# Down projection of a gated MLP: another order of the seven fast-multiplication products, sums left in PSUM, and every engine's order written by hand

## The chip, the core and the metric

The kernel runs on one core of a Trainium2 chip. The metric is the time of one execution on the device in microseconds (us), the median of the runs. The core has a matrix engine (PE, with weight loads shown apart as PEld), a vector engine (DVE), a scalar engine (ACT), a GpSimd engine (POOL) and a queue that starts transfers (SP). Each engine works through its own list of instructions in order. Results of PE go to PSUM, of which the kernel uses eight banks of 128 partitions by 512 float32; all other tiles lie in SBUF.

## The reference

One layer of a hybrid encoder on 1024 tokens of width 1024: a norm, a pooling and attention mixer with an output projection, a second norm, and a gated MLP with a causal convolution of width 3. The change touches only its last product and what follows:

```python
h = rmsnorm(x, norm_ffn_g)                       # x: 1024 x 1024, after the mixer
u = causal_dwconv(h @ w_up, conv_w, conv_b)      # w_up: 1024 x 5632
gate, val = jnp.split(u, 2, axis=-1)             # each 1024 x 2816
x = x + (jax.nn.silu(gate) * val) @ w_down       # w_down: 2816 x 1024
return rmsnorm(x, norm_final_g)
```

Everything is float32. A float32 product is done on PE as three fast passes: each operand is split into a high and a low part, and high*high, high*low and low*high are added in PSUM.

## The kernel before

The last 240 us are of interest. The activations `silu(gate) * val` come out of the up projection in 22 steps (`up`, lines 808 to 898), one for each 128 of the 2816 columns. A step holds seven products of 12 matmuls, for the up projection is done by Winograd's form of Strassen's scheme: seven block products in place of eight. The tail of a step (the taps of the convolution, the silu and the multiply, `after0` to `after4`, `store_a`, `store_b`) is done within the next step, and that of the last one behind it. `store_a` and `store_b` write the activations and three sums of them (S1 to S4) to DRAM.

The down projection uses the same scheme. The activations are cut into blocks A11, A12 (token rows 0 to 511), A21, A22 (rows 512 to 1023), the weight `w_down` into B11, B12, B21, B22, each 1408 by 512. Seven products P1 to P7 are computed, in the order P1, P2, P3, P7, P5, P6, P4 (line 975). Each has 11 units (one for 128 of the 1408 inner columns), and a unit is 4 row blocks of 128 tokens (j = 0 to 3) times the three passes of `mm3` (lines 78 to 81): 12 matmuls of 128 x 512, so that there are 7 x 11 x 12 = 924. For each unit `load` (line 979) fetches the left operand from DRAM into a `raw` tile and splits it and the right operand. A split (lines 83 to 91) is a copy on ACT for the high part (line 86) and a subtraction on DVE for the low part (line 87). Every split of the down projection is recorded at these two lines, the left ones under tile names such as aP59l, the right ones as `wP` or `lw`.

The right operands of P7, P5, P6 and P4 are sums of weight blocks. Each costs one POOL instruction per unit (`pool2`, line 956; P7 into a tile named T, the others in place in `B12`), 44 in all. Each product has four PSUM banks of its own, in turn from two pools (`banks`), begins them afresh, and when it is done, `evac` (line 1082) adds its four results into the tiles X of the residual, P5 and P7 into two places each. P1 is also copied into `sp`, P6 is added to it, and `sp` goes into three quarters of X later:

```python
elif p == "P5":
    into(x12(j), y)
    into(x22(j), y)
elif p == "P6":
    into(sp[j], y)
```

The final norm is woven into P4: for the upper 512 rows (`upper`, 4 steps each), for the lower ones partly (`lower`), and the rest in `last` (line 1070) after each of the last four groups of 9 matmuls: a square with its row sum on ACT, a multiply by the gain on DVE, two small POOL instructions for the scale of a row, the scaling of one half on DVE and the other on ACT, and two transfers out.

Order: during the up steps all engines follow an order written by hand (line 921). From line 928 on only SP does, and from line 1137 on PE; the other engines' instructions of the down projection are ordered by a planner, which may place them among those of the last up steps. Tiles come from rings of named tags (`BUFS`, line 62): `raw` has 4, `hi` and `lo` 5 each, `T` 5, `E` 6, `M` 8. A tile waits for the last reader of the tile that held its place before.

Of the kernel before, what the change touches and what calls it, by code (L numbers as in the profile page):

```python
# [50 lines left out]
def block_kernel(ctx, tc, x, xT, pos, wv, wqk, wp, wo, wup, wdn, cols, invf, rcnt, gffn, gfin,  # L51
# [723 lines left out]

    def store_b(u):
# [5 lines left out]
        tens(out=s34[:, H:T], in0=a[:, 0:H], in1=s12[:, H:T], op=sub)  # L782
        t = dram(f"S12{i}", s12)
# [24 lines left out]
    def up(p, u, g, h):  # L808
# [7 lines left out]
        product(x6, u.S2w, "T2", u.ahead)  # L816
        up_split(u, "S3", nc.gpsimd)
# [63 lines left out]
        if g:  # L881
            up_split(g, "S2")
        u.o1 = conv(u, 1, u.uv)
# [12 lines left out]
        tens(out=u.ug[:, H:T], in0=z, in1=u2, op=add)  # L896
        if p:
# [57 lines left out]
    def pool2(dst, a, b, op=sub):  # L955
        nc.gpsimd.tensor_tensor(out=dst, in0=a, in1=b, op=op)  # L956
        return dst

    t3 = {}

    def wside(p, i):
        if p in ("P1", "P2", "P3"):
            return wdown({"P1": "B11", "P2": "B21", "P3": "B22"}[p], i)
        if p == "P7":
            if i % 2 == 0:
                t3[0] = st("E", f"T3{i}")
            return pool2(t3[0][:, (i % 2) * H:(i % 2 + 1) * H], wdown("B22", i), wdown("B12", i))
        w = wdown("B12", i)
        if p == "P5":
            return pool2(w, w, wdown("B11", i))  # L970
        if p == "P6":
            return pool2(w, wdown("B22", i), w)
        return pool2(w, w, wdown("B21", i))

    left = {"P1": "A11", "P2": "A12", "P3": "S4", "P7": "S3", "P5": "S1", "P6": "S2", "P4": "A22"}
    lw = {}
    P1E = 6

    def load(p, i):
        late = p == "P4" and i >= NG - LAST  # L980
        r = st("raw", f"ar{p}{i}")
        nc.sync.dma_start(out=r, in_=opd[left[p], i])
        a = wsplit(r, f"a{p}{i}")
        if late:
            if 0 not in lw:
                lw[0] = [st("M", f"lw{k}", [P, 4, H], F32R) for k in range(2)]
            wh, wl = [t[:, i - NG + LAST, :] for t in lw[0]]
        elif p == "P4":
            if i % 2 == 0:
                lw["h"] = st("M", f"w{p}{i}", [P, 4, H], F32R)  # L990
            wh, wl = [lw["h"][:, i % 2 * 2 + k, :] for k in range(2)]
        elif i % 2 and (p != "P1" or i > P1E):
# [7 lines left out]
    def banks(p, k):  # L1000
        if k % 2 == 0:
            return [psB(f"d{p}{j}") for j in range(4)]
        t = [psS(f"d{p}{j}") for j in range(2)]
        return [t[j // 2][:, (j % 2) * H:(j % 2 + 1) * H] for j in range(4)]

    def unit(acc, j, i, w):
        c = slice(j * P, (j + 1) * P)
        mm3(acc[j], w[0][0][:, c], w[0][1][:, c], w[1][0], w[1][1], i == 0, i == NG - 1)

    def xb(j, n):  # L1010

        return lambda t: X[j * 4 + t][:, n * H:(n + 1) * H]

    x11, x12, x21, x22 = xb(0, 0), xb(0, 1), xb(1, 0), xb(1, 1)

    def into(x, y, op=add, eng=None):
        (eng or nc.vector).tensor_tensor(out=x, in0=x, in1=y, op=op)

    s3 = [sm.tile([P, 4], F32, name=f"s3{tt}", tag=f"s3{tt}", bufs=1) for tt in range(NT)]
    fin, gfb = {}, {}  # L1020

    def square(tt, n):
        if tt not in fin:
            fin[tt] = st("E", f"of{tt}")
        nc.scalar.activation(fin[tt][:, n * H:(n + 1) * H], X[tt][:, n * H:(n + 1) * H], AF.Square, accum_out=s3[tt][:, n:n + 1])

    def half_mean(tt, n):
        nc.gpsimd.tensor_scalar(out=s3[tt][:, 2:3], in0=s3[tt][:, n:n + 1], scalar1=1.0 / D, scalar2=EPS,
                                op0=ALU.mult, op1=ALU.add)

    def row_scale(tt, n):
        s = s3[tt]
        nc.gpsimd.tensor_scalar(out=s[:, 3:4], in0=s[:, n:n + 1], scalar1=1.0 / D, scalar2=s[:, 2:3],
                                op0=ALU.mult, op1=ALU.add)
# [164 lines left out]
```

## Time and profile before

| | us |
|---|---|
| median of 3 runs | 1057.57 |
| lowest, highest run | 1054.36, 1454.11 |
| the profiled execution | 1052.37 |
| its span, first to last instruction | 1050.6 |

The profiled execution is one run of its own. Its time is the span and 1.77 us outside it. The rows below are from its trace. Times are us from the start of the span. A duration ends when the result is written; the next instruction of the same engine can start earlier than that. "wP<-B12w,wP" reads: tile wP is written from B12w and wP. What stands behind "<-" in brackets is what ended an engine's idle time. PE's clock was granted in full (1.00) in every stretch of 30 us from 820 to 1030.

### The profile page before, as it was taken

How to read it: one execution, taken by the hardware profiler on the slowest of the kernel's cores; microseconds unless marked ns; L12 is line 12 of the kernel's file. 1: busy time of each engine (PE TensorE's matmuls, PEld its weight loads, DVE VectorE, ACT ScalarE, POOL GpSimd, SP SyncE). 2: the span in 40 equal slices, each digit the busy share in tenths (PEclk: the TensorE clock that was granted, in tenths of full speed). 3: DMA queues.
4: the chain of work that ended last, by engine and by line, in shares of the span. 5: the costliest groups of instructions: out<-in, count | busy, mean ns of one | idle time of the engine just before them, and what ended most of it. 6: DMA issues, size and time to landing. Idle time of an engine off the chain costs nothing.

```text
span 1050.6 us, 13509 instructions
## 1 busy us (share of the span) xinstructions
PE 1012.6 (96%) x4612; PEld 836.3 (80%) x4612; DVE 782.6 (74%) x1141; ACT 510.1 (49%) x896; POOL 324.9 (31%) x284
## 2 busy tenths in 40 slices
PE   8999999999998998999999999999999999999995
PEld 6888888887887876778888888888888788877884
DVE  6465887989775678587776777677676865799894
ACT  6722554447555355244445445454453654344533
POOL 0000121322121156443433333334332000775462
PEclk9999999999999999999999999999999999999998
DMA  9627543324325223232422322233233885533214
GB/s 313 234 90 279 182 141 120 102 71 141 117 95 180 80 85 113 73 136 78 139 100 81 121 101 100 101 118 113 72 131 130 299 313 207 163 120 112 91 65 176
DMA packets 67974, 143.89 MB, mean 137 GB/s; under 512 B 8513, under 2 KB 9665, under 8 KB 67905
## 3 DMA queue, kind: packets, MB, share of 16 engines
q1 hardware_dynamic: 67904, 143.03, 39.6%
q8 instruction: 36, 0.59, 0.2%
q14 instruction: 34, 0.27, 0.1%
HBM read 105.78 MB, written 37.22 MB: 136 GB/s over the span
## 4 chain that ended last, share of the span: by engine, by line
PE 70%; DVE 7%; POOL 3%; issue 3%; ACT 2%; DMA 1%; SPq 0%; POOLq 0%; DVEq 0%; ACTq 0%
PE P L81 9%; PE P L79 9%; PE P L80 9%; PE dP L80 4%; PE dP L81 4%; PE dP L79 4%; PE Z L79 4%; PE Z L80 4%; PE Z L81 4%; PE po L81 3%; PE po L79 3%; PE sc L386 2%; PE po L80 2%; PE O L433 2%; PE pp L79 1%
## 5 line engine op out<-in xcount | busy, mean ns | idle before, releaser
L403 POOL TENSOR_SCALAR e<-e,sm 128x128 f32<-128x128 f32 (+7 forms) x32 | 29.7, 932 | 174.9 <-DMA k<-tsk 68.9
L735 POOL TENSOR_TENSOR S<-wa,wa 128x512 f32<-128x512 f32 x44 | 64.7, 1490 | 0.9 <-DMA wa<-in_wup 0.9
L399 ACT ACTIVATE e<-sc,mx 128x128 f32<-128x128 f32 (+7 forms) x64 | 47.1, 741 | 32.5 <-DVE mx L389 16.7
L753 DVE SCALAR_TENSOR_TENSOR o<-ug,col,o 128x1023 f32<-128x1023 f32 (+1 forms) x44 | 56.3, 1281 | 0.0
L753 DVE SCALAR_TENSOR_TENSOR o<-uv,col,o 128x1023 f32<-128x1023 f32 (+1 forms) x44 | 56.3, 1279 | 0.0
L735 POOL TENSOR_TENSOR S<-S,wa 128x512 f32<-128x512 f32 x22 | 28.3, 1287 | 73.8 <-DVE a224l L87 4.8
L956 POOL TENSOR_TENSOR T<-B22w,B12w 128x512 f32<-128x512 f32 x11 | 19.0, 1728 | 93.3 <-DVE wP L87 93.3
L735 POOL TENSOR_TENSOR S<-wa,S 128x512 f32<-128x512 f32 x22 | 28.5, 1294 | 51.0 <-issue 50.9
L848 ACT COPY u<-P 128x512 f32<-128x512 f32 x18 | 10.6, 587 | 69.2 <-PE P L81 69.2
L386 PE MATMUL sc<-K,Q 128*128 128x512 f32 (+3 forms) x192 | 42.8, 352 | 0.3 <-ACT e L399 0.3
L386 PEld LDWEIGHTS sc<-K,Q 128*128 128x128 f32 x192 | 32.7, 190 | 5.7 <-ACT e L399 0.9
L748 ACT ACTIVATE o<-ug,col 128x1024 f32<-128x1024 f32 x22 | 26.6, 1210 | 20.1 <-DVE ug L896 20.1
L421 ACT COPY at<-tp 128x512 f32<-128x512 f32 (+3 forms) x48 | 21.6, 483 | 28.5 <-PE tp L417 28.5
L828 ACT COPY u<-P 128x512 f32<-128x512 f32 x18 | 10.6, 587 | 50.0 <-PE P L81 50.0
L433 PE MATMUL O<-at,V 128*128 128x256 f32 (+1 forms) x160 | 34.0, 358 | 0.0
L433 PEld LDWEIGHTS O<-at,V 128*128 128x128 f32 x160 | 29.8, 190 | 4.0
L564 DVE TENSOR_TENSOR X<-X,po 128x512 f32<-128x512 f32 x32 | 21.7, 682 | 14.7 <-PE po L81 14.6
L389 DVE TENSOR_REDUCE mx<-sc 128x1 f32<-128x640 f32 (+3 forms) x32 | 32.2, 1014 | 0.4
L806 DVE TENSOR_TENSOR ac<-o,g 128x1024 f32<-128x1024 f32 x22 | 26.9, 1224 | 7.1 <-ACT g L804 6.9
L748 ACT ACTIVATE o<-uv,col 128x1024 f32<-128x1024 f32 x22 | 26.7, 1214 | 9.6 <-DVE uv L878 9.6
L87 DVE TENSOR_TENSOR wP<-B12w,wP 128x512 fp32r<-128x512 f32 x30 | 26.4, 904 | 3.2 <-ACT wP L86 1.8
L867 ACT COPY s<-P 128x512 f32<-128x512 f32 x18 | 10.6, 587 | 33.1 <-PE P L81 33.1
(2479 smaller groups left out, 3561.2 us busy)
## 6 DMA issues: line engine op xcount, KB each, us to landing
wa<-in_wup SPq DMA_DIRECT2D x88, 256.0 KB, 3.3
S<-s SPq DMA_DIRECT2D x22, 512.0 KB, 3.0
arP<-S SPq DMA_DIRECT2D x44, 256.0 KB, 2.6
arP<-A SPq DMA_DIRECT2D x33, 256.0 KB, 5.0
Q<-q SPq DMA_DIRECT2D x64, 128.0 KB, 2.9
A<-ac SPq DMA_DIRECT2D x11, 512.0 KB, 2.9
xs<-in_x SPq DMA_DIRECT2D x8, 512.0 KB, 7.9
K<-k SPq DMA_DIRECT2D x8, 512.0 KB, 5.1
```

The lines of the kernel that those rows point to most:

```text
L79: mm(dst, lhi, rhi, start=first, stop=False, skip_group_check=more)
L80: mm(dst, lhi, rlo, start=False, stop=False, skip_group_check=more)
L81: mm(dst, llo, rhi, start=False, stop=last, skip_group_check=more)
L386: mm(sc[:, k0:k1], qst[h, grp][n * 2 + hl][:, qc], kst[h][n][:, k0:k1], start=hl == 0, stop=hl == 1)
L389: nc.vector.tensor_reduce(out=nmx[:, n:n + 1], in_=sc[:, 0:L], axis=AX.X, op=ALU.max, negate=True)
L399: nc.scalar.activation(ee[n], scs[n][:, 0:L], AF.Exp, bias=nmx[:, n:n + 1], accum_out=sums[:, n:n + 1])
L403: nc.gpsimd.tensor_scalar(out=e1, in0=e1, scalar1=sums[:, 3:4], scalar2=1.0, op0=ALU.mult, op1=ALU.mult)
L433: mm(O[:, c0:256], V[j][:, h * P:(h + 1) * P], at[:, j, c0:256], start=j == 0, stop=j == nj - 1)
L735: pool(out=t, in0=getattr(u, x), in1=getattr(u, y), op=op)
L748: nc.scalar.activation(o, src, AF.Identity, bias=col[:, cc + 3:cc + 4], scale=col[:, cc + 2:cc + 3])
L753: nc.vector.scalar_tensor_tensor(out=o[:, d:T], in0=src[:, 0:T - d], scalar=col[:, cc + 2 - d:cc + 3 - d], in1=o[:, d:T], op0=ALU.mult, op ...
L806: tens(out=p.act, in0=p.o1, in1=g, op=ALU.mult)
```

## The change

The seven products are done in the order P1, P2, P6, P5, P3, P7, P4. P1, P6, P7 and P4 use the same four banks (`xb`): P6, P7 and P4 don't begin them afresh, but go on adding, so that the banks hold P1, then P1+P6, then P1+P6+P7, then all four. P2 and P5 begin the other four banks (`zb`), and P3 adds on P5. After each product the present content of its banks is added into one place of X, 28 additions in all; `sp` and its copies are gone. P4's right operand has the opposite sign, so it is added.

The weight sums are differences now, made on DVE. During P2, B11 becomes B12-B11 (the right operand of P5). In P6, t = B22-B11, with that new B11, is the right operand, and B21 becomes B21-t (that of P4). During P3, B12 becomes B22-B12 (that of P7). That is 44 DVE instructions of 128 x 512 in SBUF: two for each unit of P6, one for each of P2 and of P3.

Every engine follows the program's order, from the first up step to the end. `prepare(k)` issues ahead: weights 5 units ahead, left operands (`fetch`) one unit before their splits (`load`), splits two units before PE needs them. The first left operands and weights are asked for inside the last up step (`first_weights(0)`), and the splits of units 0 to 4 are placed within it and between the last taps. The last activations' sums and their stores are made after units 3 and 6. X is loaded in P1 (rows 0 to 511) and in P6. The norm of the upper rows is done during P7, a first part of the lower ones during P4, and the rest after each group of 9 matmuls in two pieces: `last1` of one block comes before `last2` of the block ahead of it.

The diff, without the bodies that it moves unchanged and with its long removed stretches cut:

```diff
-        t = dram(f"A2{i}", a)
-        opd["A12", i], opd["A22", i] = t[:, 0:H], t[:, H:T]
+        if u is not us[-1]:
+            store_out1(u)
         acts["s12"] = st("E", f"s12{i}")
         tens(out=acts["s12"][:, 0:H], in0=acts[i][:, H:T], in1=a[:, H:T], op=add)
...
         s12, s34 = acts["s12"], acts["s34"]
         tens(out=s12[:, H:T], in0=s12[:, 0:H], in1=acts[i][:, 0:H], op=sub)
         tens(out=s34[:, H:T], in0=a[:, 0:H], in1=s12[:, H:T], op=sub)
+        if u is not us[-1]:
+            store_out2(u)
+    def store_out1(u):
+        i = u.f % NG
+        t = dram(f"A2{i}", u.act)
+        opd["A12", i], opd["A22", i] = t[:, 0:H], t[:, H:T]
+    def store_out2(u):
+        i, s12, s34 = u.f % NG, acts["s12"], acts["s34"]
...
-    def up(p, u, g, h):
+    def up(p, u, g, h, also=None):
...
+        if also:
+            also(0)
...
+        if also:
+            also(3)
...
+        if also:
+            also(1)
         u.o1 = conv(u, 1, u.uv)
         if p:
...
+        if also:
+            also(2)
...
-    with tc.manual_schedule(engines={E.PE, E.Activation, E.DVE, E.Pool, E.SP}):
...
+    t2 = {}
     def wside(p, i):
-        if p in ("P1", "P2", "P3"):
-            return wdown({"P1": "B11", "P2": "B21", "P3": "B22"}[p], i)
-        if p == "P7":
+        if p == "P6":
             if i % 2 == 0:
-                t3[0] = st("E", f"T3{i}")
...
+                t2[0] = st("E", f"T2{i}")
+            t = t2[0][:, (i % 2) * H:(i % 2 + 1) * H]
+            tens(out=t, in0=wdown("B22", i), in1=wdown("B11", i), op=sub)
+            tens(out=wdown("B21", i), in0=wdown("B21", i), in1=t, op=sub)
+            return t
+        return wdown({"P1": "B11", "P2": "B21", "P5": "B11", "P3": "B22", "P7": "B12", "P4": "B21"}[p], i)
+    def sums(p, i):
+        if p == "P2":
+            tens(out=wdown("B11", i), in0=wdown("B12", i), in1=wdown("B11", i), op=sub)
+        if p == "P3":
+            tens(out=wdown("B12", i), in0=wdown("B22", i), in1=wdown("B12", i), op=sub)
...
+    left = {"P1": "A11", "P2": "A12", "P6": "S2", "P5": "S1", "P3": "S4", "P7": "S3", "P4": "A22"}
+    raws, early, lw = {}, [], {}
+    def fetch(p, i):
+        r = raws[p, i] = st("raw", f"ar{p}{i}")
+        nc.sync.dma_start(out=r, in_=opd[left[p], i])
...
+    def into(j, n, y):
+        x = X[j][:, n * H:(n + 1) * H]
+        tens(out=x, in0=x, in1=y, op=add)
+    def evac(p, j, y):
+        if p in ("P1", "P2"):
+            into(j, 0, y)
+        elif p in ("P6", "P3"):
+            into(j, 1, y)
+        elif p in ("P5", "P7"):
+            into(4 + j, 1, y)
+        else:
+            into(4 + j, 0, y)
...
+    def last1(tt):
+        s = s3[tt]
         square(tt, 0)
         gain(tt, 0)
-        row_scale(tt, 0)
+        mean(s[:, 3:4], s[:, 0:1], s[:, 2:3])
+        power(s[:, 3:4])
+    def last2(tt):
...
+            emit(tt, halves[n])
...
+    todo = {}
     for j in range(4):
         for step in range(4):
-            todo[j + step].append((upper, j, step))
...
+            todo.setdefault(("P7", 1 + 2 * j + step), []).append((upper, j, step))
+        for step in range(2):
+            todo.setdefault(("P4", 1 + j + step), []).append((lower, 4 + j, step))
+    DEEP, WAHEAD = 3, 5
+    units = [(p, i) for p in left for i in range(NG)]
+    wneed = {"P1": ("B11",), "P2": ("B21", "B12"), "P6": ("B22",)}
+    xload = {("P1", 5 + k): k for k in range(4)}
+    xload.update({("P6", 4 + k): 4 + k for k in range(4)})
+    ready, ahead = {}, [0, 0, 0]
+    def prepare(k):
+        while ahead[2] < min(k + WAHEAD, len(units)):
+            p, i = units[ahead[2]]
+            for nm in wneed.get(p, ()):
+                wdown(nm, i)
+            ahead[2] += 1
+        while ahead[0] < min(k + 2, len(units)):
+            n = units[ahead[0]]
+            fetch(*n)
+            if n in xload:
+                load_x(xload[n])
+            ahead[0] += 1
+        while ahead[1] < min(k + 1, len(units)):
+            n = units[ahead[1]]
+            ready[n] = load(*n)
+            sums(*n)
+            ahead[1] += 1
+    def first_weights(step):
+        if step:
+            prepare((0, 1, 2, 0)[step])
+            return
+        early.extend(st("M", f"we{k}", [P, 4, H], F32R) for k in range(2))
+        for n in range(4):
+            fetch(*units[n])
+            wdown("B11", n)
+        ahead[0] = 4
+        for i in range(4, 8):
+            wdown("B11", i)
+    E = mybir.EngineType
+    ctx.enter_context(tc.manual_schedule(engines={E.PE, E.Activation, E.DVE, E.Pool, E.SP}))
+    for n in range(NF):
+        up(us[n - 1] if n else None, us[n], us[n + 1] if n + 1 < NF else None, us[n + 2] if n + 2 < NF else None,
+           first_weights if n == NF - 1 else None)
+    after0(us[-1])
+    prepare(3)
+    after1(us[-1])
+    after2(us[-1])
+    prepare(4)
+    after3(us[-1])
+    after4(us[-1])
...
+    xb = [psB(f"x{j}") for j in range(4)]
+    k = 0
+    for p in left:
+        if p in ("P2", "P5"):
+            t = [psS(f"d{p}{j}") for j in range(2)]
+            zb = [t[j // 2][:, (j % 2) * H:(j % 2 + 1) * H] for j in range(4)]
+        acc = zb if p in ("P2", "P5", "P3") else xb
+        more = p in ("P6", "P7", "P4", "P3")
         for i in range(NG - LAST if p == "P4" else NG):
-            while queue and len(ready) < DEEP:
...
+            prepare(k + DEEP - 1)
             w = ready.pop((p, i))
             for j in range(4):
-                unit(acc, j, i, w)
...
+                unit(acc, j, w, i == 0 and not more, i == NG - 1, more)
+                if i == NG - 1:
+                    if acc is xb:
+                        evac(p, j, acc[j])
+                    elif j % 2:
+                        evac(p, j - 1, acc[j - 1])
+                        evac(p, j, acc[j])
+            for fn, j, step in todo.get((p, i), ()):
+                fn(j, step)
+            k += 1
+            if k == 4:
+                store_a(us[-1])
+                store_b(us[-1])
+            if k == 7:
+                store_out1(us[-1])
+                store_out2(us[-1])
+        if p == "P6":
+            for n, nm in enumerate(("B21", "B12")):
+                gfb.append(wblk[nm][:, 3, :])
+                nc.sync.dma_start(out=gfb[n], in_=gfin[halves[n]].partition_broadcast(P))
+    prepare(len(units))
+    ws = [ready[("P4", i)] for i in range(NG - LAST, NG)]
+    for j in range(5):
+        if j < 4:
+            for n in range(LAST):
+                unit(xb, j, ws[n], False, n == LAST - 1, True)
+            evac("P4", j, xb[j])
+            last1(4 + j)
+        if j:
+            last2(3 + j)
```

## Rows read from the trace of the kernel before

**Rows 1.** The page: span, and busy time of each engine with its share.
```profile
span 1050.6 us, 13509 instructions
PE 1012.6 (96%) x4612; PEld 836.3 (80%) x4612; DVE 782.6 (74%) x1141; ACT 510.1 (49%) x896; POOL 324.9 (31%) x284
```
**Rows 2.** Busy times by stretch: PE, PEld, DVE, ACT, POOL, then clock, DMA.
```profile
850.00:880.00 30.00, 30.00 (x134) 24.86 (x133) 18.04 (x28) 15.55 (x28) 0.00 (x0) 1.00 0.70 240
...
910.00:940.00 30.00, 28.82 (x126) 23.21 (x125) 26.93 (x25) 11.69 (x22) 25.85 (x17) 1.00 0.44 140
940.00:970.00 30.00, 27.48 (x121) 22.10 (x120) 29.39 (x33) 13.77 (x27) 18.63 (x14) 1.00 0.33 107
```
**Rows 3.** Timeline of PE: start, duration, line, tiles; in brackets the idle time before.
```profile
804.70 0.39 PE L79 MATMUL P<-B,a1221h 128*128 128x512 f32 x1
...
814.68 0.39 PE L81 MATMUL P<-T,S321l 128*128 128x512 f32 x1
815.74 0.50 PE L79 MATMUL P<-T,a2221h 128*128 128x512 f32 x1 [0.68 <-ACT u L848]
...
829.62 0.50 PE L80 MATMUL dP<-wP,aP12h 128*128 128x512 f32 x1 [1.32 <-DVE wP L87]
...
920.05 0.50 PE L80 MATMUL dP<-wP,aP72h 128*128 128x512 f32 x1 [0.81 <-DVE wP L87]
...
947.23 0.50 PE L80 MATMUL dP<-wP,aP50h 128*128 128x512 f32 x1 [1.95 <-DVE wP L87]
...
1025.86 0.50 PE L79 MATMUL dP<-wP,aP46h 128*128 128x512 f32 x1 [1.52 <-ACT aP46h L86]
...
1039.83 0.39 PE L81 MATMUL dP<-lw,aP410l 128*128 128x512 f32 x1
```
**Rows 4.** Groups of instructions between 820 and 1051: line, engine, tiles, count, busy, mean ns.
```profile
L87 DVE TENSOR_TENSOR wP<-B12w,wP 128x512 fp32r<-128x512 f32 x30 | 26.4, 904 | 3.2 <-ACT wP L86 1.8 <-PE dP L80 1.4
L1017 DVE TENSOR_TENSOR X<-X,dP 128x512 f32<-128x512 f32 x32 | 20.6, 678 | 2.1 <-ACT sp L1084 1.4 <-PE dP L81 0.7
L956 POOL TENSOR_TENSOR T<-B22w,B12w 128x512 f32<-128x512 f32 x11 | 19.0, 1728 | 93.3 <-DVE wP L87 93.3
...
L87 DVE TENSOR_TENSOR wP<-T,wP 128x512 fp32r<-128x512 f32 x11 | 12.2, 1112 | 5.0 <-ACT wP L86 4.9
```
**Rows 5.** Timeline of DVE: start, duration, line, tiles.
```profile
806.74 0.69 DVE L782 TENSOR_TENSOR s<-ac,s 128x512 f32<-128x512 f32 x1
807.35 1.28 DVE L753 SCALAR_TENSOR_TENSOR o<-uv,col,o 128x1023 f32<-128x1023 f32 x1
808.54 0.68 DVE L742 TENSOR_TENSOR ug<-P,s 128x512 f32<-128x512 f32 x1
...
818.04 0.69 DVE L864 TENSOR_TENSOR uv<-Z,u 128x512 f32<-128x512 f32 x1
...
834.85 1.23 DVE L806 TENSOR_TENSOR ac<-o,g 128x1024 f32<-128x1024 f32 x1 [0.75 <-ACT g L804]
...
905.95 1.78 DVE L87 TENSOR_TENSOR aP70l<-arP,aP70h 128x512 fp32r<-128x512 f32 x1
```
**Rows 6.** DMA issues from 795 on: tiles, queue, count, size, median us to landing.
```profile
B11w<-in_wdn SPq DMA_DIRECT2D x11, 256.0 KB, 6.2
...
S<-s SPq DMA_DIRECT2D x4, 512.0 KB, 5.4
```
**Rows 7.** Timeline of DVE in the last 17 us.
```profile
1034.11 0.69 DVE L1017 TENSOR_TENSOR X<-X,dP 128x512 f32<-128x512 f32 x1 [0.66 <-PE dP L81]
...
1041.92 0.68 DVE L1017 TENSOR_TENSOR X<-X,dP 128x512 f32<-128x512 f32 x1
```
**Rows 8.** Timeline of ACT in the last 17 us.
```profile
1037.08 0.72 ACT L1076 ACTIVATE of<-of,s 128x512 f32<-128x512 f32 x1 [1.52 <-POOL s L1035]
1037.71 0.61 ACT L1025 ACTIVATE of<-X 128x512 f32<-128x512 f32 x1
...
1045.65 0.72 ACT L1076 ACTIVATE of<-of,s 128x512 f32<-128x512 f32 x1 [1.52 <-POOL s L1035]
```

More of the change, by code (lines that the diff above doesn't have):

```diff
@@ L1016, in into, with unit @@
-    def into(x, y, op=add, eng=None):
-        (eng or nc.vector).tensor_tensor(out=x, in0=x, in1=y, op=op)
+    def unit(acc, j, w, first, last, more):
+        c = slice(j * P, (j + 1) * P)
+        mm3(acc[j], w[0][0][:, c], w[0][1][:, c], w[1][0], w[1][1], first, last, more)
+    def into(j, n, y):
[10 more added lines that the diff above has]
+            into(4 + j, 0, y)
@@ new lines, in power, with emit, upper @@
+    def power(s):
+        nc.gpsimd.tensor_tensor(out=s, in0=s, in1=nhalf[:, 0:1], op=ALU.pow)
+    def emit(tt, ns):
+        nc.sync.dma_start(out=out[tt * P:(tt + 1) * P, ns], in_=fin[tt][:, ns])
+    halves = (slice(0, H), slice(H, T))
+    def upper(tt, step):
+        s = s3[tt]
+        if step == 0:
+            square(tt, None)
+        elif step == 1:
+            mean(s[:, 3:4], s[:, 0:1], EPS)
+            power(s[:, 3:4])
+        elif step == 2:
+            fin[tt] = st("E", f"of{tt}")
+            for n in range(2):
+                nc.vector.scalar_tensor_tensor(out=fin[tt][:, halves[n]], in0=X[tt][:, halves[n]], scalar=s[:, 3:4],
+                                               in1=gfb[n], op0=ALU.mult, op1=ALU.mult)
+        else:
+            emit(tt, slice(0, T))
@@ L1037, in gain, with lower @@
[L1037 to L1044 removed]
+        tens(out=fin[tt][:, halves[n]], in0=X[tt][:, halves[n]], in1=gfb[n], op=ALU.mult)
+    def lower(tt, step):
+        s = s3[tt]
         if step == 0:
[L1047 removed]
             square(tt, 1)
@@ L1049, in upper @@
         elif step == 1:
-            row_scale(tt, 1)
-        elif step == 3:
-            emit(tt, slice(0, T))
-        else:
-            for n in range(2):
-                ns = slice(n * H, (n + 1) * H)
-                nc.vector.scalar_tensor_tensor(out=fin[tt][:, ns], in0=X[tt][:, ns], scalar=s3[tt][:, 3:4],
-                                               in1=gfb[n], op0=ALU.mult, op1=ALU.mult)
-    def lower(j, step):
-        if step == 0:
-            into(x22(j), sp[j])
-            square(4 + j, 1)
-        elif step == 1:
-            into(x21(j), sp[j], eng=nc.gpsimd)
-            half_mean(4 + j, 1)
-        elif step == 2:
-            gain(4 + j, 1)
@@ L1070, in last @@
-    def last(tt):
+            mean(s[:, 2:3], s[:, 1:2], EPS)
+            gain(tt, 1)
+    def last1(tt):
+        s = s3[tt]
         square(tt, 0)
         gain(tt, 0)
-        row_scale(tt, 0)
+        mean(s[:, 3:4], s[:, 0:1], s[:, 2:3])
+        power(s[:, 3:4])
+    def last2(tt):
         o, s = fin[tt], s3[tt]
@@ L1117, in block_kernel @@
             w = ready.pop((p, i))
             for j in range(4):
-                unit(acc, j, i, w)
-            if p == "P4":
-                for fn, j, step in todo.pop(0):
-                    fn(j, step)
-            if p == "P6" and i < 4:
-                square(i, 0)
-                half_mean(i, 0)
-        if p in ("P2", "P7"):
-            n = int(p == "P7")
-            t = gfb[n] = wblk["B12" if n else "B21"][:, 3, :]
-            nc.sync.dma_start(out=t, in_=gfin[n * H:(n + 1) * H].partition_broadcast(P))
@@ L1131, in block_kernel @@
-        if p != "P4":
-            while queue and len(ready) < DEEP:
-                n = queue.pop(0)
-                ready[n] = load(*n)
-            for j in range(4):
-                evac(p, j, acc[j])
-    ctx.enter_context(tc.manual_schedule(engines={mybir.EngineType.PE}))
-    ws = [ready.get(("P4", i)) or load("P4", i) for i in range(NG - LAST, NG)]
-    for fn, j, step in sum(todo, []):
-        fn(j, step)
-    for j in range(4):
-        for n, i in enumerate(range(NG - LAST, NG)):
-            unit(acc, j, i, ws[n])
-        evac("P4", j, acc[j])
-        last(4 + j)
+                unit(acc, j, w, i == 0 and not more, i == NG - 1, more)
```

111 lines of the change are left out of this document (17 added, 94 removed).

## The prediction

> **What bounds the kernel now.** I read the page first: PE is busy 96% of the span [rows 1], so an edit around the same matmuls can only win back PE's idle time and what follows its last matmul. The page can't say where these lie. The busy times by stretch can: 850 to 880 PE is full, while from 910 to 940 and from 940 to 970 it misses 1.2 and 2.5 us, and there DVE is busy 26.9 and 29.4 of 30 and POOL 25.9 and 18.6 [rows 2]. So the down projection has places in which its feeders are the limit. The timeline of PE gives the size.
>
> Its pace: from 804.70 to 814.68 lie 44 matmul steps, 0.2268 us each [rows 3]; a unit of 12 is 2.72, a product 29.9. At 815.74 the last but one product of the up projection starts. From there to the end PE has 12 + 12 + 924 = 948 matmuls, 215.0 us at that pace, which would end at 1030.75. The last one starts at 1039.83, so its slot ends at 1040.06: **9.3 us are lost** in the down projection. The brackets name the large pieces: 1.32 at 829.62, 0.81 at 920.05, 1.95 at 947.23, all until a right operand's low part on DVE, and 1.52 at 1025.86 until a copy on ACT [rows 3]; smaller waits and the slow restart behind each make the rest. The second loss is the end: from 1040.06 to the span's end are 10.5 us.
>
> Why DVE is late around 920 to 955 the groups show: a subtraction of 128 x 512 is 0.69 us when alone [rows 5], but the same form has a mean of 0.904 (wP from B12w) and 1.112 (wP from T) in this part, and single ones last 1.78 [rows 4, 5]. These are the stretches in which POOL adds weight blocks at 1.73 each [rows 4].
>
> **The matmuls.** The products keep 924 matmuls of the same shape; beginning a bank or going on adding is the same instruction. Cost 0, and 215.0 us remain the floor from 815.74.
>
> **POOL's 44 sums go, 44 on DVE come.** What DVE pays is not the 0.69 of a row but the distance to the next start: 806.74 to 807.35 is 0.61 [rows 5], so I take 0.60 to 0.61 for 128 x 512 and 1.2 for a tap (807.35 to 808.54 [rows 5]). A unit has two low parts, 1.2 us. In P2 and P3 one sum makes it 1.8, in P6 two make it 2.4: below PE's 2.72 everywhere. P6 is the tight one: 11 x 2.4 = 26.6, and the four additions of P2's banks, 2.4, make 29.0 against 29.9. In P6 DVE also waits for ACT's copy of t, which runs beside the update of B21; a few hundredths per unit would stay in the margin of 0.3. I take 0.3 us of lost PE time; bounds 0 and 3.2 (the durations as occupancy, rival A). Cover: splits run two units, 5.4 us, ahead; without it P6's start shows each lateness.
>
> The Trainium skill speaks against this move, in "VectorE: DVE Perf Modes", section on the TRN2 errata: a float32 add of two tensors is put at 691 ns for 512 elements. The rows agree with that as a duration (0.69 in rows 5). Taken as what each instruction occupies, P6 would be over PE's pace; the starts 0.61 apart say that it is not. By the page's figure the time would be rival A's.
>
> **Additions into X.** Before, 11 per row block counting those of `sp`, with a copy on ACT; after, 7. At 0.68 [rows 4] the 16 that go on DVE or POOL were beside PE's work; I give them no time. Where banks are used again at once, PE waits for them: P4 goes on in P7's banks, P3 in P5's. P7 to P4: bank j is read while PE does the other three row blocks, 2.04 us, and the reading takes 0.68 if DVE is free. P5 to P3 they are read in pairs behind row blocks 1 and 3: 1.36 us for two readings of 0.6 to 0.68, which just fits. I take 0.2, bounds 0 and 1.4 (both readings in full, twice).
>
> **The start.** PE's last product of the up projection ends at 815.74 + 24 x 0.2268 = 821.2. DVE's list after 818.04 (uv) [rows 5] is now: uv, unit 0, the multiply of the step before, unit 1, s34, ug, unit 2, a tap, unit 3, two taps, unit 4, a tap, a wait for silu (I take 1.3), the multiply, unit 5, three sums, unit 6. At 0.6 and 1.2 the steps end so: ug 823.4, unit 2 824.6, unit 3 827.0, unit 4 830.6, the multiply 834.3, unit 5 835.5, unit 6 838.5. PE wants unit n at 821.2 + 2.72 n: unit 2 at 826.6, 3 at 829.4, 4 at 832.1 are in time; unit 5 (834.8) is 0.7 late, unit 6 then 0.3, and the fourth bank, which ug reads until 823.4, 0.3 late for row block 3 (823.2). Sum 1.3, in place of some 2 lost there now (the 1.32 at 829.62 and its sides); bounds 0 and 3 (a tap and a multiply more on the path).
> Transfers: the tiles of B11 take over those of an operand whose last matmuls are the nine from 804.70 [rows 3], free at 806.8; 6.2 us to landing [rows 6] is 813, before 818.7. The unit 9 weights take the tile of s34, whose store is issued behind unit 6 (about 838.5) and needs 5.4 [rows 6]: 844 plus the split 1.2 against 821.2 + 1.3 + 24.5 = 847.0. ACT stands still until then with units 9 and 10 queued behind it, so this one has a margin of some 2 us. I give it 0.2; bounds 0 and 2.
>
> **The end.** Now the four last blocks run as a loop (square, two POOL steps, scaling; 1045.65 is three rounds after 1037.08, 2.86 us each [rows 8]): ACT scales one block (1037.08) before it squares the next (1037.71), while PE needs 9 x 0.2268 = 2.04 for a block, so that the last addition starts at 1041.92 [rows 7] though PE's data are there at 1040.22. The change puts the square of a block ahead of the scaling of the one before, so the last block's chain starts with PE. From addition to the end of scaling: 1034.11 to 1037.80, 3.7 us [rows 7, 8]. From the end of the last scaling, 1046.37 [rows 8], to the span's end are 4.2. With 0.2 from the end of PE's slot to the addition: 8.1 in place of 10.5, **2.4 us** gained; bounds 0 and 2.4.
>
> **Sum.** Losses kept: 0.3 + 0.2 + 1.3 + 0.2 = 2.0, so 7.3 of 9.3 come back. Span 1030.75 + 2.0 + 8.1 = 1040.85; with 1.77 outside it 1042.6, 9.8 less than the profiled 1052.37. Of the shown times 1052.37, 1054.36 and 1057.57 lie together; the middle one is 2.0 above the profiled one, and I add this: 1044.6, **1045**. Best case: all losses 0, 1042.6. All upper bounds at once: 9.6 lost and the old end, 1030.75 + 9.6 + 10.5 + 1.8 + 2.0 = 1054.7. Half of it is more likely than the whole, so the forecast's own range is 1041 to 1051.
>
> **Rivals.**
> A. DVE bounds P6: at 0.69 an instruction a unit is 2.76 (over 2.72), and with the 4 additions 33.1 against 29.9. With nothing ready ahead that costs 3.2, 1048. For: two dependent sums in a row, and a copy on ACT between them and the low part. Against: starts 0.61 apart, 5.4 us ahead. The Trainium skill's "VectorE: DVE Perf Modes" (the TRN2 errata) would give this, as occupancy.
> B. The time comes back as waits in a fixed order: a transfer holds ACT, and both splits queued behind it. The old kernel has one such wait of 1.52 at 1025.86 [rows 3]; six of them, one at each change of product, undo 9.3: about 1054. Against: the left operands are asked for a unit before their splits, and after P6 only 256 KB per unit are read.
> C. Slower: DVE instructions stay as long as now, though POOL is quiet. At 1.112 [rows 4] P6 takes 4.45 a unit, 19.0 over PE, and P2 and P3 3.34 a unit, 13.6 over: 1044.6 + 32.6 = 1077. It decides from about 0.9 an instruction, where P6 alone loses 11 x (3.6 - 2.72) = 9.7 and cancels the gain. For: that is the mean measured, 0.904 [rows 4]. Against: the long ones stand where POOL adds, and POOL keeps only 128 x 1 steps and one split. The Trainium skill's "Perfetto Trace Analysis", on optimizing Scalar/DVE operations, is for taking work off a saturated DVE, and adds that POOL shares a port with it, so that this may not help; the 1.78 beside POOL's adds bear out the second half.
> D. The change does more or less than it says: the planner, which orders everything before the up steps, may order that differently with another tail. Nothing in the diff touches it; 5 us either way, at most.
>
> **How the numbers follow.** Forecast 0.68, A 0.12, B 0.12, C 0.05, D 0.03. The range 1039 to 1055 holds the forecast with its bounds, A and B, and leaves out C and parts of D, B and the forecast's ends, below 2 in 10. About 2%, 21 us, is what a measurement of this kernel can tell from no change. All cases but C and a freak of D lie within it: even without a single lost us the down projection gives 11.7, so faster by over 2% is 0.03, slower by over 2% 0.05 and within 0.92.
>
> **What would show it.** PE's timeline from 850 on without idle brackets over 0.3 us; DVE's low parts at 0.69 with none at 1.78; in P6 four DVE instructions per 2.72 us with idle time between them; the start's waits around 835; the last square within 1 us of PE's last matmul. I am wrong if P6's units are more than 2.72 apart, if ACT waits for transfers between 838 and 850, or if the last addition starts much later than PE's end.

## The result, and the profile after

The changed kernel takes 1045.11 us (median of 6 runs, 1043.27 to 1046.32), the kernel before 1057.41 in the same sessions. One run before, 1454.11, lies far above the others and is left out of the ratio. The ratio is 0.9889, with a 95% interval of 0.9873 to 0.9906: 1.1% faster, clear of noise, and inside the 2% that were named as the bound. The forecast was 1045, with 1039 to 1055.

The profiled execution took 1043.27 us. Its page, span and busy times [rows 1]:

```profile
span 1041.4 us, 13413 instructions
PE 1012.4 (97%) x4612; PEld 837.6 (80%) x4612; DVE 763.8 (73%) x1169; ACT 507.0 (49%) x884; POOL 241.8 (23%) x232
```

The busy times by stretch, columns as in [rows 2]:

```profile
850.00:880.00 30.00, 30.00 (x134) 24.86 (x133) 26.04 (x43) 13.58 (x24) 0.00 (x0) 1.00 0.93 322
880.00:910.00 30.00, 30.00 (x134) 24.85 (x133) 28.53 (x46) 12.97 (x24) 0.00 (x0) 1.00 0.52 176
910.00:940.00 30.00, 30.00 (x134) 24.82 (x134) 17.59 (x28) 13.54 (x25) 0.00 (x0) 1.00 0.33 105
940.00:970.00 30.00, 29.89 (x132) 24.48 (x131) 22.52 (x38) 12.58 (x22) 0.00 (x0) 1.00 0.30 97
```

Where PE missed 1.2 and 2.5 of 30 us it now misses 0 and 0.1, and POOL does nothing there. DVE's own columns can't be set side by side, for the products stand in another order: P6 with its 22 sums lies mostly in 880 to 910, where DVE is busy 28.5 of 30 and PE is full all the same, and 910 to 940 holds no sum. Over the whole compared part, from the row at 817.33 (815.74 before) to PE's last slot, DVE is busy 164.2 us in place of 181.6, with 256 instructions in place of 227.

PE's timeline, with every place from 816 on where its starts fall behind the pace by more than 0.2 us, and its last matmul [rows 3]:

```profile
817.33 0.50 PE L79 MATMUL P<-T,a2221h 128*128 128x512 f32 x1 [0.68 <-ACT u L860]
...
820.45 0.47 PE L79 MATMUL Z<-B,S421h 128*128 128x512 f32 x1
...
840.31 0.50 PE L80 MATMUL x<-wP,aP16h 128*128 128x512 f32 x1 [0.21 <-DVE wP L87]
...
943.87 0.47 PE L79 MATMUL dP<-wP,aP30h 128*128 128x512 f32 x1
...
1033.49 0.39 PE L81 MATMUL x<-wP,aP410l 128*128 128x512 f32 x1
```

The row at 817.33 is the point from which the prediction counted (815.74 before). From there 948 matmuls at 0.2268 would end at 1032.33; the last slot ends at 1033.72. So 1.4 us are lost where 9.3 were: 0.34 at 820.45, 0.47 at 840.31 and 0.34 at 943.87, each with its restart; the rest is the restart behind 817.33 and drift.

The two executions do not start the compared part at the same time, 815.74 and 817.33, though none of PE's work ahead of it was edited. All traces are therefore compared below from their own row of this kind to the end of their span. The new kernel's end is 1041.4, the old one's 1050.6: **224.1 us against 234.9**, 10.8 less. Of these 7.9 are PE's lost time and 2.9 the end behind the last slot (7.7 in place of 10.5).

In P6, the tight product, DVE's timeline of one unit and the start of the next:

```profile
887.83 0.68 DVE L87 TENSOR_TENSOR aP63l<-arP,aP63h 128x512 fp32r<-128x512 f32 x1
888.43 0.69 DVE L969 TENSOR_TENSOR T<-B22w,B11w 128x512 f32<-128x512 f32 x1
889.15 0.69 DVE L970 TENSOR_TENSOR B21w<-B21w,T 128x512 f32<-128x512 f32 x1
889.80 0.69 DVE L87 TENSOR_TENSOR wP<-T,wP 128x512 fp32r<-128x512 f32 x1
890.41 0.68 DVE L87 TENSOR_TENSOR aP64l<-arP,aP64h 128x512 fp32r<-128x512 f32 x1
```

A unit takes 2.58 (887.83 to 890.41), just under PE's 2.72: starts are 0.60 to 0.65 apart, but 0.72 where an instruction reads what the one ahead of it writes (888.43 to 889.15). The end, first DVE, then ACT, then POOL:

```profile
1033.91 0.69 DVE L1011 TENSOR_TENSOR X<-X,x 128x512 f32<-128x512 f32 x1 [0.23 <-PE x L81]
1034.63 0.69 DVE L1063 TENSOR_TENSOR of<-X,B21w 128x512 f32<-128x512 f32 x1
1035.24 0.48 DVE L1083 TENSOR_SCALAR of<-of,s 128x512 f32<-128x512 f32 x1
```
```profile
1034.69 0.60 ACT L1031 ACTIVATE sq<-X 128x512 f32<-128x512 f32 x1 [0.70 <-DVE X L1011]
...
1036.52 0.72 ACT L1084 ACTIVATE of<-of,s 128x512 f32<-128x512 f32 x1 [0.49 <-POOL s L1037]
```
```profile
1035.52 0.34 POOL L1034 TENSOR_SCALAR s<-s 128x1 f32<-128x1 f32 x1 [1.07 <-ACT sq L1031]
```

The last addition starts 0.2 behind PE's last slot (1.9 before [rows 7]); the last scaling ends at 1037.24, 3.5 behind the slot (6.3 before [rows 8]). The gain of a block (L1063) runs beside its square (L1031).

### The profile page after: what moved, and what is told of

It is laid out like the page before. It is cut to its first block, busy times and chain, and to the rows that moved or that the text cites. A ratio compares the mean times of both kernels' runs of the same rounds, so it can differ in the third digit from the quotient of the medians.

```text
span 1041.4 us, 13413 instructions
## 1 busy us (share of the span) xinstructions
PE 1012.4 (97%) x4612; PEld 837.6 (80%) x4612; DVE 763.8 (73%) x1169; ACT 507.0 (49%) x884; POOL 241.8 (23%) x232
## 4 chain that ended last, share of the span: by engine, by line
PE 76%; DVE 5%; issue 2%; DMA 2%; ACT 1%; POOL 1%; POOLq 0%; SPq 0%; DVEq 0%; ACTq 0%
PE P L81 9%; PE P L79 9%; PE P L80 9%; PE Z L79 4%; PE Z L80 4%; PE Z L81 4%; PE x L80 3%; PE x L81 3%; PE x L79 3%; PE dP L79 3%; PE dP L81 3%; PE dP L80 3%; PE po L81 3%; PE po L79 3%; PE po L80 3%; PE sc L386 3%
## 5 line engine op out<-in xcount | busy, mean ns | idle before, releaser
L1034 POOL TENSOR_SCALAR s<-s 128x1 f32<-128x1 f32 x12 | 4.8, 403 | 217.4 <-ACT sq0None L1031 167.5
L735 POOL TENSOR_TENSOR S<-wa,S 128x512 f32<-128x512 f32 x22 | 28.5, 1294 | 51.7 <-issue 51.6
L748 ACT ACTIVATE o<-ug,col 128x1024 f32<-128x1024 f32 x22 | 26.6, 1210 | 18.2 <-DVE ug L912 18.2
L748 ACT ACTIVATE o<-uv,col 128x1024 f32<-128x1024 f32 x22 | 26.7, 1215 | 10.3 <-DVE uv L892 10.3
L814 ACT ACTIVATE g<-o 128x1024 f32<-128x1024 f32 x22 | 22.6, 1029 | 13.0 <-DVE o L753 12.9
```

Of the source, the lines that this page charges most:

```text
L735: pool(out=t, in0=getattr(u, x), in1=getattr(u, y), op=op)
L748: nc.scalar.activation(o, src, AF.Identity, bias=col[:, cc + 3:cc + 4], scale=col[:, cc + 2:cc + 3])
```

## The experiments

Each is the changed or the old kernel with one edit. "Part" is the time from the last but one up product to the end of the span: 234.9 before, 224.1 changed. Ratios are to the kernel before, run on the same chip; a PE loss is counted against the pace of 0.2268, with the restart.

**1. The weight sums back on POOL.**

```diff
-            tens(out=t, in0=wdown("B22", i), in1=wdown("B11", i), op=sub)
-            tens(out=wdown("B21", i), in0=wdown("B21", i), in1=t, op=sub)
+            pool(out=t, in0=wdown("B22", i), in1=wdown("B11", i), op=sub)
+            pool(out=wdown("B21", i), in0=wdown("B21", i), in1=t, op=sub)
```
(and the sums in P2 and P3 likewise)

> The changed kernel with its 44 weight sums on POOL again, all else as changed. Theory (POOL's adds stretch DVE's low parts and take longer than a unit leaves): P6 has two POOL adds of 1.5 to 1.7 us per unit, 3.2 to 3.4 against PE's 2.72, and DVE low parts beside them last up to 1.78; P6 alone loses 5 to 9 us, so 1050 to 1054. Rival (the order by hand is what won, the sums don't matter): 1044 to 1046, PE without gaps in P6.

1051.71 us, ratio 0.9951 (0.9934 to 0.9967); part 230.5, 6.4 more than the changed kernel. PE's waits come back, most in P6 (3.9 us over four units), some in P2 and one in P1. From PE's timeline:

```profile
843.64 0.50 PE L80 MATMUL x<-wP,aP16h 128*128 128x512 f32 x1 [1.27 <-DVE wP L87]
...
882.38 0.50 PE L80 MATMUL dP<-wP,aP29h 128*128 128x512 f32 x1 [0.36 <-DVE wP L87]
...
897.33 0.50 PE L80 MATMUL x<-wP,aP62h 128*128 128x512 f32 x1 [1.72 <-DVE wP L87]
```

POOL's and DVE's timelines at the last of them:

```profile
895.47 1.26 POOL L969 TENSOR_TENSOR T<-B22w,B11w 128x512 f32<-128x512 f32 x1 [0.41 <-PE x L81]
896.81 1.61 POOL L970 TENSOR_TENSOR B21w<-B21w,T 128x512 f32<-128x512 f32 x1
```
```profile
894.83 0.77 DVE L87 TENSOR_TENSOR aP62l<-arP,aP62h 128x512 fp32r<-128x512 f32 x1
895.53 1.75 DVE L87 TENSOR_TENSOR wP<-T,wP 128x512 fp32r<-128x512 f32 x1
897.20 1.77 DVE L87 TENSOR_TENSOR aP63l<-arP,aP63h 128x512 fp32r<-128x512 f32 x1
```

The time is the theory's, and so are the stretched low parts, but not the split of the loss (P6 alone loses 3.9 where 5 to 9 was given) and not its other reason, that POOL's adds don't fit into a unit. POOL ran far ahead (it did its first P6 sum at 868, 20 us early) and was at the tenth of the eleven units when the waits stopped. What PE waited for were low parts of 1.75 while POOL was adding. The row at 843.64 shows the same in P1: a sum of the last activations on DVE took 1.71, beside a POOL sum made early for P2.

**2. The old order at the end.**

```diff
             last1(4 + j)
-        if j:
-            last2(3 + j)
+            last2(4 + j)
```

> The changed kernel with the two scalings and transfers of a block right behind its own square again. Theory (ACT's order makes a loop per block longer than PE's 2.04 us): with the loop at 2.55 (its POOL steps are shorter now than before) the last block is 3 x 0.5 = 1.5 us late, up to 2.5 if the POOL steps go back to 0.76; 1046.5 to 1047.5. Rival (the end hangs on the last transfer alone): no change, 1045.

1047.04 us, ratio 0.9903 (0.9886 to 0.9920); part 226.7, 2.7 more. ACT's timeline at the end:

```profile
1035.18 0.60 ACT L1031 ACTIVATE sq<-X 128x512 f32<-128x512 f32 x1 [0.46 <-DVE X L1011]
...
1036.94 0.72 ACT L1084 ACTIVATE of<-of,s 128x512 f32<-128x512 f32 x1 [1.03 <-POOL s L1037]
1038.12 0.60 ACT L1031 ACTIVATE sq<-X 128x512 f32<-128x512 f32 x1 [0.45 <-DVE X L1011]
```

That last line should be read with its wait: the square waits for the addition, which stands behind the scaling in DVE's list. So a block takes 2.94 (1035.18 to 1038.12), not the 2.55 of the theory, and the last scaling is 6.2 behind PE's last slot. The theory's loop is there, but it goes through DVE as well as ACT, and costs more than expected.

**3. The planner orders ACT, DVE and POOL again,** and PE up to the last four blocks.

```diff
-    ctx.enter_context(tc.manual_schedule(engines={E.PE, E.Activation, E.DVE, E.Pool, E.SP}))
-    for n in range(NF):
+    with tc.manual_schedule(engines={E.PE, E.Activation, E.DVE, E.Pool, E.SP}):
+        for n in range(NF):
...
+    ctx.enter_context(tc.manual_schedule(engines={E.SP}))
...
+    ctx.enter_context(tc.manual_schedule(engines={E.PE}))
```

> The changed kernel, but ACT, DVE and POOL ordered by the planner from the first product of the down projection on, as in the kernel before (SP by hand, PE by hand for the last blocks). Theory: without POOL's sums the planner's order costs PE 0 to 3 us more and the end 0 to 2.4; 1045 to 1050. Rival (the order by hand is the whole gain): 1053 to 1056.

1049.84 us, ratio 0.9925 (0.9908 to 0.9941); part 228.3, 4.2 more. The end is unchanged (3.5). PE loses 4.4 us more (5.7 in place of 1.4), at three places; the two large ones on its timeline, 3.2 and 1.8 with the restarts:

```profile
839.66 1.20 PE L79 MATMUL x<-wP,aP15h 128*128 128x512 f32 x4 [2.63 <-ACT wP L86]
...
894.38 0.50 PE L80 MATMUL x<-wP,aP62h 128*128 128x512 f32 x1 [1.50 <-DVE wP L87]
```

So the order by hand is worth 4 us, at the start and at the beginning of P6; it is not the whole gain.

**4. The kernel before, its sums on DVE.**

```diff
-        nc.gpsimd.tensor_tensor(out=dst, in0=a, in1=b, op=op)
+        nc.vector.tensor_tensor(out=dst, in0=a, in1=b, op=op)
```

> The kernel before with one edit: its 44 weight sums on DVE in place of POOL. Theory: low parts fall to 0.69, the waits between 910 and 960 (0.81, 0.37, 1.95, 0.57 and the restarts, near 4.8 us) go, the start and the end stay: 4 to 5 us faster than before. Rival (the order decides): within 1 us of before. Rival (DVE gets too full): P5 with its 8 additions and a sum per unit loses more than now, slower by 1 to 4.

1051.60 us, ratio 0.9953 (0.9935 to 0.9971); part 230.1, 4.8 less than before. The busy times by stretch:

```profile
910.00:940.00 30.00, 30.00 (x134) 24.80 (x133) 28.82 (x48) 13.69 (x25) 0.00 (x0) 1.00 0.50 167
940.00:970.00 30.00, 30.00 (x134) 24.84 (x133) 25.47 (x42) 14.07 (x28) 7.21 (x3) 1.00 0.32 105
```

PE is full in both stretches. DVE does 48 instructions in the first in place of 25 [rows 2] in hardly more time. One word in the old kernel removes all four waits between 910 and 960, and no low part lasts over 0.69 any more. The waits at the start and near the end stay: PE still loses 4.6 us, 2.0 of it in P1 and 2.3 in P4, and the end behind its last slot is 10.5 as before.

**5. The kernel before, with the new order at the end alone.**

```diff
-        evac("P4", j, acc[j])
-        last(4 + j)
+            evac("P4", j, acc[j])
+            last(4 + j)
+        if j:
+            last2(3 + j)
```
(ACT, DVE and POOL by hand from there; `last2` holds the scalings and transfers)

> The kernel before with one edit: in the last four blocks the scalings and transfers of a block come behind the square of the next one, in the order of the program. Theory: the last scaling ends 3.3 to 3.7 us behind PE's last slot instead of 6.3; from the start of the last but one up product to the end 234.9 becomes 232.2 to 232.6, and the time 2 to 3 us less than before (ratio 0.997 to 0.998). Rival (something else in the old order delays the last block, such as DVE's gains): 0 to 1 us.

1055.81 us, ratio 0.9994 (0.9983 to 1.0005): no gain that can be measured. Its part is 234.8, against 234.9. The last scaling ends 4.9 behind PE's last slot, so half of the expected 2.8 is there at that point. DVE's timeline and POOL's:

```profile
1045.48 0.67 DVE L1017 TENSOR_TENSOR X<-X,dP 128x512 f32<-128x512 f32 x1
1046.93 0.69 DVE L1039 TENSOR_TENSOR of<-X,B21w 128x512 f32<-128x512 f32 x1 [0.79 <-ACT of L1025]
```
```profile
1047.00 0.76 POOL L1033 TENSOR_SCALAR s<-s 128x1 f32<-128x1 f32 x1 [1.05 <-ACT of L1025]
```

The gain (L1039) waits 0.79 for the square, which in the old kernel writes into the tile that the gain writes next, and the next addition stands behind the gain. The changed kernel also lets the square write into PSUM, an edit that the prediction had not costed. That explains the missing half. The half that is there doesn't show in the part either: 1.0 us of it is left at the end of the span, and PE lost 10.2 us in this execution where it lost 9.3 before, by a longer wait and a lower clock at 924.79 (last section). The interval of the ratio does not exclude 1 us. The theory, as it stood, falls.

**6. and 7. The other half of the end.** In experiment 6 the changed kernel's lower squares write into the output tile again; in 7 the kernel before has both edits. The line that matters, and the opposite in 7:

```diff
-        junk = psS(f"sq{tt}{n}")
+        if n is None:
+            junk = psS(f"sq{tt}{n}")
+        else:
+            if tt not in fin:
+                fin[tt] = st("E", f"of{tt}")
+            junk = fin[tt]
```

> The changed kernel with the squares of the lower rows written into the tile of the output again (SBUF, as in the kernel before) instead of into PSUM; order unchanged. Theory (the gain on DVE then waits for the square, and the next addition behind it, and POOL's first step falls beside the gain): a block takes 2.48 us as in the kernel before with the new order alone, the last one 1.3 late, the POOL step 0.4 longer; last scaling 5.0 to 5.3 us behind PE's last slot instead of 3.5, 1.5 to 1.8 us slower than the changed kernel. Rival (order alone makes the end): 3.5 us as before, no change.

1047.88 us, ratio 0.9904 (0.9887 to 0.9922); part 225.8, 1.7 more; the last scaling 4.9 behind the slot.

> The kernel before with both edits of the end: scalings behind the next block's square, and the lower rows' squares written into PSUM. Theory: the last scaling 3.5 us behind PE's last slot instead of 6.3, 2.8 us less than before (ratio 0.9965 to 0.998). Rival (the end of the old kernel hangs on something else): as with the order alone, 4.9 us and 0 to 1.5 us less.

1053.63 us, ratio 0.9964 (0.9952 to 0.9976); part 233.0, 1.9 less than before and not 2.8, for PE lost 10.2 in this execution too; the last scaling 3.5 behind the slot (ACT's timeline; PE's last slot ends at 1044.31):

```profile
1047.11 0.72 ACT L1084 ACTIVATE of<-of,s 128x512 f32<-128x512 f32 x1 [0.49 <-POOL s L1039]
```

From the slot to the last scaling: old order and old target 6.3, new order alone 4.9, new target alone 6.2 (experiment 2), both 3.5. To the end of the span, with the last transfers: 10.5, 9.6 and 9.4 (experiments 5 and 6), 10.3, and 7.7 to 7.8. Each edit needs the other: with the old order the addition stands behind the scaling, with the old target behind the square.

**8. One more DVE instruction in each unit of P6.**

```diff
-            tens(out=t, in0=wdown("B22", i), in1=wdown("B11", i), op=sub)
+            for _ in range(2):
+                tens(out=t, in0=wdown("B22", i), in1=wdown("B11", i), op=sub)
```

> The changed kernel with one more DVE instruction of 128 x 512 in each unit of P6 (t is made twice). Theory (a unit of P6 takes DVE 2.6 of 2.72 us): with 3.2 a unit DVE bounds P6; the splits are 0.6 us ahead in unit 2 and 1.6 in unit 10, so PE loses 3.5 to 4.5 us, 1049. Rival (splits run far enough ahead to hide it): 0 to 1. Rival (an instruction occupies DVE for its 0.69): 5 or more, and already the changed kernel would wait in P6, which its trace does not show.

1049.23 us, ratio 0.9934 (0.9922 to 0.9946); part 228.3, 4.2 more. PE waits in each unit from unit 4 to unit 10 (the last), about 0.55 with the restart; two of the seven on its timeline:

```profile
896.55 0.49 PE L80 MATMUL x<-wP,aP64h 128*128 128x512 f32 x1 [0.23 <-DVE wP L87]
...
906.48 0.50 PE L80 MATMUL x<-wP,aP67h 128*128 128x512 f32 x1 [0.23 <-DVE wP L87]
```

In the changed kernel P6's units of 2.58 to 2.67 were 0.05 to 0.14 us away from being bound by DVE.

**9. Splits one unit ahead instead of two.** `DEEP, WAHEAD = 2, 5`.

> The changed kernel with splits one unit ahead instead of two (DEEP 2). Theory: only where additions into X come before the splits of a dense product does PE wait, 1 to 2 us at the start of P6, under 1 elsewhere: 1046 to 1048. Rival (two units ahead is what closes the gaps everywhere): PE waits at each of the six changes of product, 6 us or more, 1051 or more.

1049.41 us, ratio 0.9936 (0.9920 to 0.9951); part 227.0, 2.9 more. PE's timeline:

```profile
839.11 0.50 PE L80 MATMUL x<-wP,aP15h 128*128 128x512 f32 x1 [1.95 <-DVE wP L87]
...
889.37 0.50 PE L80 MATMUL x<-wP,aP61h 128*128 128x512 f32 x1 [0.23 <-DVE wP L87]
```

Waits at two places, not at each change of product: 1.3 at the start of P6, as expected, and 2.2 at unit 5 of P1 in place of 0.5 at unit 6, which was not: its splits now stand behind the sums of the last activations. The time, read by the ratios, is some 5 us more, with an uncertainty of more than 2; the trace shows 2.9.

**10. Each addition into X twice, except those of P4** (so the output holds these products twice).

```diff
     def evac(p, j, y):
+        evac1(p, j, y)
+        if p != "P4":
+            evac1(p, j, y)
```

> The changed kernel with each addition into X done twice, except those of P4, so 24 more DVE additions of 128 x 512 from PSUM (the output has those products twice). Theory (the additions lie beside PE's work, except where a bank is used again at once): P5 to P3 loses about 1.5 us (four readings of 0.65 against 1.36), P2 to P6 another 1 to 2, the rest nothing; 1047 to 1049. Rival (each addition costs PE time): 24 x 0.65 = 15, 1060. Rival (all hidden): 1045.

1051.32 us, ratio 0.9958 (0.9946 to 0.9970); part 231.4, 7.3 more. PE's timeline, where it waits for banks:

```profile
950.35 0.47 PE L79 MATMUL dP<-wP,aP30h 128*128 128x512 f32 x1 [1.55 <-DVE X L1011]
...
952.89 0.50 PE L79 MATMUL dP<-wP,aP30h 128*128 128x512 f32 x1 [0.94 <-DVE X L1011]
...
1013.84 0.51 PE L79 MATMUL x<-wP,aP40h 128*128 128x512 f32 x1 [0.35 <-DVE X L1011]
```

Neither rival holds, and the theory only in part. Of its two places, P2 to P6 loses what was said (1.35, behind a longer list of DVE), P5 to P3 twice as much (3.0: eight readings follow one another, so both pairs are late). Two places that it had put at nothing lose 3.1: P1 to P2 1.45, behind a longer list, and P7 to P4 1.6. There the four banks, doubled, take 5.4 us to read, while PE needs the last of them 4.1 us (six row blocks of 0.68) after the first is done.

**11. and 12. The last activations' sums a unit later** (`if k == 5` in place of `if k == 4`), in two runs; the first gives a trace alone.

> The changed kernel with the three sums of the last activations made behind unit 4 instead of unit 3 of P1 (so behind the splits of unit 6). Theory (PE's wait of 0.2 at unit 6 is DVE's list, 1.8 us of sums ahead of these splits): that wait goes, the 0.5 us with its restart, and no other appears, since unit 7 has 1 us of room. Rival (the wait is a late transfer): it stays.

Part 223.5, and PE's wait at unit 6 is gone with no other in its place.

> The changed kernel with the last activations' sums behind unit 4, timed. Theory: 0.5 us under the changed kernel (ratio 0.9884 against its 0.9889), too little for this measurement to tell; from the start of the last but one up product to the end 223.5, against 224.1 of the changed kernel. Rival: nothing gained, 224.1.

1044.39 us, ratio 0.9885 (0.9862 to 0.9908); part 223.5 again. The traces show the 0.5 us twice; the times can't tell this kernel from the changed one.

## Why the prediction was right, step by step

**PE's lost time.** 2.0 us were to stay of 9.3; 1.4 stayed. P6 lost nothing (0.3 given), the changes of product 0.3 (0.2 given), unit 9 nothing (0.2 given). Units 5 and 6 lost 0.5 where 1.0 was given, and the fourth bank nothing where 0.3 was given: the list of DVE came in the order and nearly at the times worked out (multiply, then unit 5 done at 837.0, 19.7 after the row at 817.33; 19.8 by the working), but PE was itself some 0.4 later by then. The 0.3 at 820.45, a part of that, had not been seen: PE's next product waits for DVE's reading of its bank. DVE's timeline, that reading and the end of unit 5:

```profile
819.62 0.69 DVE L876 TENSOR_TENSOR uv<-Z,u 128x512 f32<-128x512 f32 x1
...
836.31 0.69 DVE L87 TENSOR_TENSOR wP<-B11w,wP 128x512 fp32r<-128x512 f32 x1
```

**Two signs that came out otherwise.** A wait of ACT for transfers between 838 and 850 was named as a sign of being wrong. It came, longest for the left operand of unit 10 and not for the weights of unit 9, and PE lost nothing by it, so the sign was badly chosen. And DVE was to have idle time between its instructions in P6 and had none: behind the four additions at 882.60 it ran without a pause to the end of P6's splits. ACT's timeline, then DVE's:

```profile
847.19 0.62 ACT L86 CAST aP110h<-arP 128x512 fp32r<-128x512 f32 x1 [4.53 <-DMA arP<-A]
```
```profile
882.60 2.64 DVE L1011 TENSOR_TENSOR X<-X,dP 128x512 f32<-128x512 f32 x4 [0.96 <-PE dP L81]
```

**The sums.** The main step holds from both sides: moving them alone gives the old kernel 4.8 (experiment 4), moving them back costs the new one 6.4 (experiment 1). In the old kernel that is half of all that PE lost. Rival C did not come: no low part of the changed kernel lasts over 0.69. The Trainium skill's "Perfetto Trace Analysis", on optimizing Scalar/DVE operations, warned that work shared between DVE and POOL may gain nothing because of a common port; experiment 1's 1.75 beside POOL's adds, 0.69 without, bears out that it gains nothing, and here it is worse than nothing; that a port is the reason no row shows.

**DVE's pace.** Taken from starts 0.61 apart; P6's unit was put at 2.4 and took 2.58 to 2.67, since dependent instructions start 0.72 apart. The margin was less than half of the 0.3 that I gave it, and still enough; experiment 8 shows that it was real, and that DVE is the limit right behind it. (11 x 2.4 is 26.4 and not the 26.6 of the working; nothing hangs on it.) The 691 ns of the Trainium skill's "VectorE: DVE Perf Modes" (TRN2 errata) is the duration of these rows too, but four of them fit into 2.58, so rival A's reading of it as occupancy is wrong here.

**The end.** 8.1 was forecast and 7.7 came. The size was right and the reason half right: the step "the change puts the square of a block ahead of the scaling of the one before, so the last block's chain starts with PE" holds only with the square in PSUM. The order alone gives 1.45 of 2.8 by the last scaling, and 1.0 of 2.9 by the end of the span (experiments 5 to 7). The chain was also shorter than the 3.7 taken over, 3.33: POOL's first step took 0.34 and not 0.76, with the gain done before it began.

**Additions.** Before there were 12 per row block and not 11, for POOL makes one more, so 20 go and not 16; the step gave them no time, and that holds. Experiment 4 keeps all 48, and PE is full in every stretch from 850 to 1000. The 28 that stay are free except for the 0.34 at 943.87 (P5 to P3); experiment 10 shows how near P7 to P4, too, is to costing.

**Order by hand.** Rival B (waits in a fixed order) did not come; experiment 3 shows the opposite, 4.2 us for the order. Experiments 4 and 3 and the end don't simply add up: the parts share the start and the change to P6. Counted from experiment 4, the sums are 4.8 of the 10.8; of the other 6.0, 2.8 are the end and 3.2 what is left over of PE's waits in P1 and P4 against the changed kernel's. For these 3.2 the order by hand is the likely cause (experiment 3 brings a wait in P1 back); the order of the products and the earlier fetching were not tested alone.

**Sum and base.** 10.8 like for like against 9.8 forecast. The forecast 1045 and the measured 1045.11 agree better than the steps do, and that is luck: the part came out 1.0 shorter than forecast, and it began 1.6 later for a reason that no edit made (last section). The profiled execution of before was quick: its compared part began at 815.74, in the three other traces of the old kernel's forms between 818.74 and 819.14, with the same work ahead of it. Adding 2.0 to go from that execution to a median was too little for the old kernel (5.0) and right for the new one (1.8).

## What to carry to other kernels

Look at the duration of one instruction form across stretches before moving work: where it doubles beside another engine, that engine's help can cost more than it gives, and taking over its work can free the one that takes it. For a loop at the end, write down for each engine what stands behind the instruction that waits: an order and a scratch target each closed the same loop here, and only both edits opened it. And where a feeder fills 95% of the matrix engine's pace, cost dependent pairs by their own distance, not by that of independent ones.

## What the runs showed of the hardware

- **The clock behind a wait.** At 418.3 PE restarts in both kernels after 3.5 us without work, with the same instructions. The busy times by stretch, clock third from the right, first the changed kernel, then the one before:

```profile
420.00:424.00 4.00, 4.00 (x10) 3.08 (x10) 1.21 (x1) 0.35 (x1) 3.17 (x3) 0.50 0.49 149
```
```profile
420.00:424.00 4.00, 4.00 (x15) 3.18 (x15) 2.11 (x3) 0.33 (x1) 3.10 (x3) 0.81 0.51 163
```

The clock (0.50 is 1.2 of 2.4 GHz) came back some 3.4 us later in the changed kernel (near 424.9 and 421.5, by stretches of 1 us). The same matmul stands at 404.66 and 404.73 ahead of this and at 427.21 and 425.62 behind it: 1.7 us between the two executions, which no edit made. In experiment 5 a wait of 2.16 in the down projection was followed by a stretch at a lower clock, on PE's timeline and by stretch:

```profile
924.79 0.73 PE L80 MATMUL dP<-wP,aP72h 128*128 128x512 f32 x1 [2.16 <-DVE wP L87]
```
```profile
925.00:930.00 5.00, 5.00 (x16) 3.92 (x17) 5.00 (x5) 1.76 (x3) 4.17 (x3) 0.67 0.30 108
```

It cost about 1.5 us (16 matmuls in 5 us for 24 in the next stretch of that length, part of it the restart). In experiment 7 the wait before 951 did the same; in the kernel before a wait of 1.95 at 947.23 did not [rows 3], nor did one of 2.63 in experiment 3. So the old kernel's waits cost some executions more than their length, which may be why the medians differ by more than the traces; that was not tested.
- **In the last four blocks a small POOL instruction of 128 x 1 took 0.67 to 0.76 where DVE's gain (two inputs from SBUF) ran beside it, and 0.26 to 0.34 where the gain was done.** It is the same form: the old kernel and experiments 4 to 6 against the changed kernel and experiment 7. Nothing was run that changes this overlap alone.
